# A fp32 encoder trunk on one core: the order of the matmuls in the MLP's first product, and where group C's query norm is applied

## The chip, the cores and the metric

One core of a Trainium2 chip runs the whole program. The metric is the device time of one execution in microseconds, lower is better; a kernel's time is the median of its runs.

## The reference, cut to what matters

Two layers (DEPTH 2) over one sequence of 256 tokens and a model width of 2048, all in float32:

```python
h = rmsnorm(x, norm_mix[l]); proj = h @ w_in[l]           # 2048 -> 3840: q, k, v of the groups A, B, C
oa = window_attention(...); ob = neighborhood_attention(...); oc = axial_global_attention(qc, kc, vc, ...)
x = x + concat(rmsnorm(oa), rmsnorm(ob), rmsnorm(oc)) @ w_o[l]
h = rmsnorm(x, norm_mlp[l])
u = relu(h @ w_up[l])                                       # 2048 -> 8192
x = x + (u * u) @ w_down[l]                                 # 8192 -> 2048

# group C: 16 query heads, 4 key heads, 64 wide
q = axial_rope(rmsnorm(q, q_gain), ...); k = axial_rope(rmsnorm(k, k_gain), ...)
p = softmax((q @ k.T) * 64 ** -0.5); o = p @ v
```

After the two layers a last rmsnorm follows. rmsnorm of a query head divides its 64 numbers by one root mean square, so it is one factor for each token and head.

## The kernel before, in words

Weights come from HBM in steps of 512 KB (`wraw`, 128 x 1024 elements). For each step ScalarE rounds them to `whi` (L803), VectorE takes the rest `wlo = wraw - whi` (L804), and TensorE runs products of the halves; activations are kept as a pair of halves too (`hT`, `hT2`, `mixT`, `uT`). The list `steps` sets the order of the weights: the input projection in eight chunks (`IN_CHUNKS`: qa, kva, kvc, qc0, qc1, vb, b0, b1), the output projection, then the MLP. Loads run seven steps ahead and splits two. Three of the products are run: high x high, high x low, low x high.

In the input and output projections and in the MLP's second product (`mode_b`, L449 to L451) the activations are the stationary operand and 512 weight columns stream: three matmuls of 512 columns for each 128 rows of weights. In the MLP's first product (`up_steps`) it is the other way round: a 128 x 128 block of weights is stationary and the tokens stream. One step has two k-blocks (`kk`) of 128 rows and four blocks of 128 output features (`fs`), each with a PSUM bank of its own (`box["b"][fs]`). For the high half of the weights both halves of the 256 tokens stream in one matmul of 512 columns (L614), and for the low half only the tokens' high half, 256 columns (L616), into the first 256 columns of the same bank. There are 8 steps for each of 16 feature chunks and 2 layers: 256 steps, 512 k-blocks, 2048 matmuls of each kind.

Attention is woven in between the weights' matmuls: a planner (`add`, `tick`) keeps pieces of work (`q_transposes` L246, `k_transposes` L261, `unit_scores` L324/L325, `unit_transp` L365, `unit_pv` L384/L377) with a cost and a delay in its own units, and releases them between steps. Its numbers do not change here. A unit is four heads by 128 queries; each layer has 8 units of C, 4 of A and 4 of B. The framework then settles each engine's order, which is fixed before the program runs; each engine works through its own list in order.

Group C's queries and keys go through `rope(raw, H, which, l, outs)` when their chunk of the projection ends: squares (L284) and their sums (L286) on VectorE; then, on GpSimd, mean plus epsilon (L288), the power -0.5 (`rsqrt`, L236), the product of `raw` with that factor (L291), and the rotary products with a cosine and a sine table (L297, L301), added at L509 into `qs`, which `q_transposes` reads. In a unit of C, VectorE takes the negative row maximum of the scores (L332), ScalarE the exponentials (L346), VectorE a reciprocal (L354) and GpSimd the product (L356).

Of the kernel before, what the change touches and what calls it, by code (L numbers as in the profile page):

```python
# [43 lines left out]
def tile_trunk(ctx: ExitStack, tc: tile.TileContext, x_in, w_in, w_o, w_up, w_down,  # L44
# [19 lines left out]
    def big(dt, *shape):  # L64
        return dp.tile([P, *shape], dt, tag="big", bufs=24, name=nm("big"))
# [168 lines left out]
    def rsqrt(ms, n):  # L234
        r = small(n)
        nc.gpsimd.tensor_tensor(r, ms, mhalf[:, 0:n], op=ALU.pow)  # L236
        return r
# [41 lines left out]
    def rope(raw, H, which, l, outs):  # L279

        n = NT * H
        sq = big(F32, NT * H * 64)
        flat = raw.rearrange("p t h d -> p (t h d)")
        nc.vector.tensor_mul(sq, flat, flat)  # L284
        s = small(n)
        nc.vector.tensor_reduce(s, sq.rearrange("p (a d) -> p a d", d=64), axis=AX.X, op=ALU.add)  # L286
        ms = small(n)
        nc.gpsimd.tensor_scalar(ms, s, 1.0 / 64, EPS, op0=ALU.mult, op1=ALU.add)  # L288
        r = rsqrt(ms, n)
        rv = raw.rearrange("p t h d -> p (t h) d")  # L290
        nc.gpsimd.tensor_mul(rv, rv, r.rearrange("p (a o) -> p a o", o=1).to_broadcast([P, n, 64]))  # L291
        t1 = big(F32, NT, H, 64)
        ct, st = ctab[which, l], stab[which, l]
        t2 = sq.rearrange("p (t h d) -> p t h d", t=NT, h=H)
        for t in range(NT):
            cb = ct[:, t:t + 1, :].to_broadcast([P, H, 64])
            nc.gpsimd.tensor_mul(t1[:, t, :, :], raw[:, t, :, :], cb)  # L297
            for a in range(4):
                b = a ^ 1
                sb = st[:, t:t + 1, 16 * a:16 * a + 16].to_broadcast([P, H, 16])  # L300
                nc.gpsimd.tensor_mul(t2[:, t, :, 16 * a:16 * a + 16], raw[:, t, :, 16 * b:16 * b + 16], sb)  # L301
            outs(t, t1[:, t, :, :], t2[:, t, :, :])


    class Unit:
# [12 lines left out]
    def unit_scores(u):  # L318
# [11 lines left out]
        if u.kind == "C":  # L330
            for b in range(2):
                nc.vector.tensor_reduce(negm[:, 2 * b:2 * b + 2], S[b], axis=AX.X, op=ALU.max, negate=True)  # L332
            src = [S[s // 2][:, s % 2, :] for s in range(4)]
        else:
            for b in range(2):
                nc.vector.scalar_tensor_tensor(p[:, 2 * b:2 * b + 2, :], S[b], 0.125,
                                               u.bias(b), op0=ALU.mult, op1=ALU.add)
            if u.kind == "A":
                nm0 = small(4)
                nc.vector.tensor_reduce(nm0, p, axis=AX.X, op=ALU.max, negate=True)  # L340
                nc.vector.tensor_tensor(negm, nm0, negsink[:, u.l, 4 * u.kv:4 * u.kv + 4], op=ALU.min)
            else:
                nc.vector.tensor_reduce(negm, p, axis=AX.X, op=ALU.max, negate=True)
            src = [p[:, s, :] for s in range(4)]
        for s in range(4):
            nc.scalar.activation(p[:, s, :], src[s], AF.Exp, bias=negm[:, s:s + 1],  # L346
                                 accum_out=sums[:, s:s + 1])
        if u.kind == "A":
            es = small(4)
# [105 lines left out]
    def layer_steps(l):  # L455
# [12 lines left out]
        def proj_evac(name, banks):  # L468
# [32 lines left out]
            elif name in ("qc0", "qc1"):  # L501
# [5 lines left out]

                def outs(t, a, b):
                    nc.gpsimd.tensor_add(qs[:, t, :].rearrange("p (h d) -> p h d", h=8), a, b)  # L509
                rope(raw, 8, "q", l, outs)  # L510
                i = int(name[2])
                kh, kl = st["k"]["C"]
                for g in range(2):
                    qT = big(F32R, 4, 256)
                    pq = add(lambda g=g, qT=qT: q_transposes(qs, 2 * g, qT), 0.45, delay=D_RQ)
                    for qb in range(2):
                        queue_unit(g_unit(l, st, "C", 2 * i + g, qb, qT, kh, kl, st["V"]["C"]), pq, st["kC"])
            elif name == "qa":
                qs = big(F32, NT, 512)
                for t in range(NT):  # L520
# [74 lines left out]
        def up_steps(g):  # L595
            for c in range(2):
                fc = 2 * g + c
                box = {}
                for k in range(8):
# [3 lines left out]
                    def mm(wh, wl, k=k, fc=fc, box=box):  # L603
# [2 lines left out]
                        ht = st["hT2"][k]  # L606
                        for kk in range(2):
                            for fs in range(4):
                                o = box["b"][fs]
                                s0 = k == 0 and kk == 0  # L610
                                s1 = k == 7 and kk == 1
                                sh = wh[:, kk, fs * P:(fs + 1) * P]
                                sl = wl[:, kk, fs * P:(fs + 1) * P]
                                nc.tensor.matmul(o.rearrange("p (s c) -> p s c", s=2), sh, ht[:, :, kk, :],  # L614
                                                 start=s0, stop=False, skip_group_check=True)
                                nc.tensor.matmul(o[:, 0:256], sl, ht[:, 0, kk, :],  # L616
                                                 start=False, stop=s1, skip_group_check=True)
                        if k == 7:
                            for b in range(2):

# [108 lines left out]
                                        ap=[[1, P], [512, 4], [1, 384]]))  # L729
        return tb  # L730

    def g_unit(l, st, kind, kv, qb, qT, kh, kl, V, bias=None):
        u = Unit()
        u.kind, u.l, u.kv, u.qb, u.qT, u.kh, u.kl, u.V = kind, l, kv, qb, qT, kh, kl, V
        u.slot = lambda s: (s, kv, qb)
        u.col = lambda s: s
# [224 lines left out]
```

## Time and profile before

| | |
|---|---|
| time, median of 3 runs (lowest to highest) | 2074.8 us (2074.34 to 2076.07) |
| the profiled execution: time, span | 2079.03 us, 2077.2 us |
| mean granted TensorE clock | 0.997 |
| PE busy | 2054.9 us, 99% of the span, 10423 matmuls |
| DVE, ACT, POOL busy | 1358.6, 1044.6, 274.4 us |
| DMA | 381.26 MB, mean 184 GB/s |

PE is TensorE's matmuls and PEld its weight loads, DVE is VectorE, ACT ScalarE, POOL GpSimd. The span runs from the first to the last instruction of the profiled execution. A matmul's recorded duration includes the time in which it fills and drains the array, and the next one starts before it ends, so what a matmul costs in a stream is the distance from its start to the next one's start, not its duration.

### The profile page before, as it was taken

The page shows a single profiled execution, that of the slowest core. Times are in us where ns is not written, and L with a number is a line of the kernel's source. Part 1 is how long each engine was busy: PE and PEld are TensorE (multiplying, and loading weights), DVE is VectorE, ACT ScalarE, POOL GpSimd, SP SyncE. Part 2 cuts the span into 40 slices and gives each one's busy share as a digit, 9 for nine tenths or more (in the row PEclk, how much of TensorE's full clock was granted, in tenths as well). Part 3 has the DMA queues.
Part 4 walks back from the last instruction along what each step waited for, and adds up shares of the span by engine and source line. Part 5 has one row for each costly group of instructions (what it writes and reads, how often), then busy time and mean ns, then how long its engine had stood idle before and what let it go on. Part 6 is the DMA issues. An engine that isn't in the chain of part 4 may idle for free.

```text
span 2077.2 us, 27421 instructions
## 1 busy us (share of the span) xinstructions
PE 2054.9 (99%) x10423; PEld 1739.5 (84%) x10423; DVE 1358.6 (65%) x1635; ACT 1044.6 (50%) x1538; POOL 274.4 (13%) x298
## 2 busy tenths in 40 slices
PE   9999999999999999999999999999999999999998
PEld 7878788888888888888888787888888888888887
DVE  6887976565565555656668889766565556656565
ACT  6657656444344443444556666555344444434444
POOL 0485420000000000000005843200000000000001
PEclk9999999999999999999999999999999999999999
DMA  7655465565666666566556453555666666666663
GB/s 283 180 159 152 152 193 174 189 191 187 193 186 190 191 189 193 186 193 189 186 183 184 148 163 118 193 173 190 191 186 193 192 185 192 190 190 188 192 212 123
DMA packets 107681, 381.26 MB, mean 184 GB/s; under 512 B 11891, under 2 KB 14707, under 8 KB 107548
## 3 DMA queue, kind: packets, MB, share of 16 engines
q1 hardware_dynamic: 107116, 378.41, 58.1%
q8 instruction: 82, 1.34, 0.3%
q10 hardware_dynamic: 432, 1.10, 0.1%
q14 instruction: 51, 0.42, 0.1%
HBM read 377.34 MB, written 2.11 MB: 183 GB/s over the span
## 4 chain that ended last, share of the span: by engine, by line
PE 92%; DVE 3%; POOL 3%; issue 1%; DMA 1%; ACT 1%; SPq 0%; POOLq 0%; DVEq 0%
PE mm L614 23%; PE mm L450 18%; PE mm L449 18%; PE mm L451 18%; PE mm L616 12%; PE tr L365 1%; DVE wlo L804 1%; PE tr L192 1%; PE mm L324 1%; PE mm L325 1%; POOL big L301 1%; DVE big L268 1%; POOL big L356 0%; POOL big L509 0%; DMA biasB<-in_rpb_dram 0%
## 5 line engine op out<-in xcount | busy, mean ns | idle before, releaser
L804 DVE TENSOR_TENSOR wlo<-wraw,whi 128x1024 fp32r<-128x1024 f32 (+1 forms) x697 | 867.2, 1246 | 654.8 <-ACT whi L803 652.3
L803 ACT CAST whi<-wraw 128x1024 fp32r<-128x1024 f32 (+1 forms) x697 | 730.1, 1050 | 914.3 <-PE mm L451 476.7
L614 PE MATMUL mm<-big,whi 128*128 128x512 f32 x2048 | 724.4, 399 | 0.0
L449 PE MATMUL mm<-whi,big 128*128 128x512 f32 (+1 forms) x1800 | 698.1, 389 | 2.4 <-ACT whi L803 1.4
L450 PE MATMUL mm<-wlo,big 128*128 128x512 f32 (+1 forms) x1800 | 695.7, 387 | 0.6 <-DVE wlo L804 0.4
L451 PE MATMUL mm<-whi,big 128*128 128x512 f32 (+1 forms) x1800 | 694.8, 386 | 0.0
L616 PE MATMUL mm<-big,wlo 128*128 128x256 f32 x2048 | 576.0, 281 | 0.0
L614 PEld LDWEIGHTS mm<-big,whi 128*128 128x128 f32 x2048 | 385.4, 188 | 95.2
L449 PEld LDWEIGHTS mm<-whi,big 128*128 128x128 f32 x1800 | 339.2, 189 | 68.7 <-DVE x L586 2.2
L451 PEld LDWEIGHTS mm<-whi,big 128*128 128x128 f32 x1800 | 339.2, 188 | 67.8
L450 PEld LDWEIGHTS mm<-wlo,big 128*128 128x128 f32 x1800 | 339.7, 189 | 66.2 <-DVE wlo L804 2.3
L616 PEld LDWEIGHTS mm<-big,wlo 128*128 128x128 f32 x2048 | 387.8, 189 | 0.5
L236 POOL TENSOR_TENSOR sm<-sm,mhalf 128x2 f32<-128x2 f32 (+3 forms) x16 | 23.7, 1482 | 785.9 <-DVE sm L231 772.0
L356 POOL TENSOR_SCALAR big<-big,sm 128x256 f32<-128x256 f32 x128 | 95.9, 767 | 224.4 <-DVE sm L354 199.7
L699 POOL TENSOR_TENSOR x<-x,big 128x512 f32<-128x512 f32 x6 | 8.6, 1453 | 722.7 <-ACT mid L706 722.7
L651 DVE SCALAR_TENSOR_TENSOR x<-mm,sm,x 128x512 f32<-128x512 f32 x127 | 89.2, 743 | 3.1 <-PE mm L451 3.1
L624 ACT COPY mid<-mm 128x256 f32<-128x256 f32 x128 | 46.7, 374 | 26.7 <-PE mm L616 26.7
L625 DVE TENSOR_TENSOR mid<-mid,mm 128x256 f32<-128x256 f32 x128 | 49.5, 420 | 0.0
L626 DVE SCALAR_TENSOR_TENSOR mid<-mid 128x512 f32<-128x512 f32 x64 | 44.0, 688 | 1.1
L630 DVE TENSOR_TENSOR big<-mid,big 128x512 fp32r<-128x512 f32 x64 | 43.8, 684 | 0.0
L367 DVE TENSOR_TENSOR big<-tr,big 128x512 fp32r<-128x512 f32 x64 | 41.1, 680 | 0.8 <-ACT big L366 0.5
L629 ACT CAST big<-mid 128x512 fp32r<-128x512 f32 x64 | 40.2, 627 | 2.6
(119 smaller groups left out, 1006.7 us busy)
## 6 DMA issues: line engine op xcount, KB each, us to landing
wraw<-in_w_up_dram SPq DMA_DIRECT2D x256, 512.0 KB, 3.5
wraw<-in_w_down_dram SPq DMA_DIRECT2D x256, 512.0 KB, 3.5
wraw<-in_w_in_dram SPq DMA_DIRECT2D x119, 512.0 KB, 3.6
wraw<-in_w_o_dram SPq DMA_DIRECT2D x64, 512.0 KB, 3.8
biasB<-in_rpb_dram SPq DMA_DIRECT2D x16, 349.5 KB, 6.3
biasA<-avec SPq DMA_DIRECT2D x4, 768.0 KB, 6.7
x<-in_x_dram SPq DMA_DIRECT2D x3, 512.0 KB, 8.7
big<-in_gfin_dram SPq DMA_DIRECT2D x2, 512.0 KB, 4.5
```

What stands on the lines that cost most here:

```text
L356: nc.gpsimd.tensor_scalar(p[:, s, :], p[:, s, :], rs[:, s:s + 1], 1.0, op0=ALU.mult, op1=ALU.mult)
L449: nc.tensor.matmul(o, a_h, wh[:, i, :], start=first and i == 0, stop=False)
L450: nc.tensor.matmul(o, a_h, wl[:, i, :], start=False, stop=False)
L451: nc.tensor.matmul(o, a_l, wh[:, i, :], start=False, stop=last and i == len(sub) - 1)
L614: nc.tensor.matmul(o.rearrange("p (s c) -> p s c", s=2), sh, ht[:, :, kk, :], start=s0, stop=False, skip_group_check=True)
L616: nc.tensor.matmul(o[:, 0:256], sl, ht[:, 0, kk, :], start=False, stop=s1, skip_group_check=True)
L624: nc.scalar.copy(ai, o[:, 256:512])
L625: nc.vector.tensor_add(ai, ai, o[:, 0:256])
L626: nc.vector.scalar_tensor_tensor(a, a, 0.0, a, op0=ALU.max, op1=ALU.mult)
L651: nc.vector.scalar_tensor_tensor(xs, box["b"][t], st["r2"][:, t:t + 1], xs, op0=ALU.mult, op1=ALU.add)
L803: last_hi[0] = nc.scalar.copy(h[:, part], w[:, part]).ins
L804: nc.vector.tensor_sub(lo[:, part], w[:, part], f(h[:, part]))
```

## The change

Three things. In `up_steps` each k-block first runs the four 512-column matmuls of its four feature blocks and then the four of 256 columns. In `rope` the squares are taken by an activation on ScalarE, for queries and keys. And for queries the factor r is no longer multiplied into `raw`: the rotary products are made of the raw queries, r is worked out behind them on GpSimd, is handed to the units as `rq`, and comes in at the softmax: the negative maximum is multiplied by it on VectorE, and the exponential takes it as its scale. Keys keep their order. `t2` gets a tile of its own, where it shared that of the squares.

```diff
@@ rope
-        nc.vector.tensor_mul(sq, flat, flat)
+        nc.scalar.activation(sq, flat, AF.Square, bias=zero1[:, 0:1])
         s = small(n)
         nc.vector.tensor_reduce(s, sq.rearrange("p (a d) -> p a d", d=64), axis=AX.X, op=ALU.add)
         ms = small(n)
-        nc.gpsimd.tensor_scalar(ms, s, 1.0 / 64, EPS, op0=ALU.mult, op1=ALU.add)
-        r = rsqrt(ms, n)
-        rv = raw.rearrange("p t h d -> p (t h) d")
-        nc.gpsimd.tensor_mul(rv, rv, r.rearrange("p (a o) -> p a o", o=1).to_broadcast([P, n, 64]))
+        if which == "k":
+            nc.gpsimd.tensor_scalar(ms, s, 1.0 / 64, EPS, op0=ALU.mult, op1=ALU.add)
+            r = rsqrt(ms, n)
+            rv = raw.rearrange("p t h d -> p (t h) d")
+            nc.gpsimd.tensor_mul(rv, rv, r.rearrange("p (a o) -> p a o", o=1).to_broadcast([P, n, 64]))
         t1 = big(F32, NT, H, 64)
+        t2 = big(F32, NT, H, 64)
...
+        if which == "k":
+            return
+        nc.gpsimd.tensor_scalar(ms, s, 1.0 / 64, EPS, op0=ALU.mult, op1=ALU.add)
+        r = sp.tile([P, n], F32, tag="rq", bufs=3, name=nm("rq"))
+        nc.gpsimd.tensor_tensor(r, ms, mhalf[:, 0:n], op=ALU.pow)
+        return r
@@ unit_scores, kind C
                 nc.vector.tensor_reduce(negm[:, 2 * b:2 * b + 2], S[b], axis=AX.X, op=ALU.max, negate=True)
+            nc.vector.tensor_mul(negm, negm, u.rq)
...
             nc.scalar.activation(p[:, s, :], src[s], AF.Exp, bias=negm[:, s:s + 1],
+                                 scale=u.rq[:, s:s + 1] if u.kind == "C" else 1.0,
                                  accum_out=sums[:, s:s + 1])
@@ up_steps
                         for kk in range(2):
                             for fs in range(4):
-                                o = box["b"][fs]
-                                s0 = k == 0 and kk == 0
-                                s1 = k == 7 and kk == 1
                                 sh = wh[:, kk, fs * P:(fs + 1) * P]
+                                nc.tensor.matmul(box["b"][fs].rearrange("p (s c) -> p s c", s=2), sh, ht[:, :, kk, :],
+                                                 start=k == 0 and kk == 0, stop=False, skip_group_check=True)
+                            for fs in range(4):
                                 sl = wl[:, kk, fs * P:(fs + 1) * P]
-                                nc.tensor.matmul(o.rearrange("p (s c) -> p s c", s=2), sh, ht[:, :, kk, :],
-                                                 start=s0, stop=False, skip_group_check=True)
-                                nc.tensor.matmul(o[:, 0:256], sl, ht[:, 0, kk, :],
-                                                 start=False, stop=s1, skip_group_check=True)
+                                nc.tensor.matmul(box["b"][fs][:, 0:256], sl, ht[:, 0, kk, :],
+                                                 start=False, stop=k == 7 and kk == 1, skip_group_check=True)
```

The changed kernel's lines stand 1 to 10 numbers further down: L614 and L616 of before are L621 and L625 there, and GpSimd's L297, L301 and L509 are L298, L302 and L518.

TensorE, the first k-block of the first MLP step, before (mm are the four banks, big the tokens, whi and wlo the halves of the weights):

```order
L614 MATMUL mm_3346<-big_3193,whi_3298 128x512
L616 MATMUL mm_3346<-big_3193,wlo_3299 128x256
L614 MATMUL mm_3347<-big_3193,whi_3298 128x512
L616 MATMUL mm_3347<-big_3193,wlo_3299 128x256
L614 MATMUL mm_3348<-big_3193,whi_3298 128x512
L616 MATMUL mm_3348<-big_3193,wlo_3299 128x256
L614 MATMUL mm_3349<-big_3193,whi_3298 128x512
L616 MATMUL mm_3349<-big_3193,wlo_3299 128x256
```

The same k-block in the changed kernel:

```order
L621 MATMUL mm_3355<-big_3202,whi_3307 128x512
L621 MATMUL mm_3356<-big_3202,whi_3307 128x512
L621 MATMUL mm_3357<-big_3202,whi_3307 128x512
L621 MATMUL mm_3358<-big_3202,whi_3307 128x512
L625 MATMUL mm_3355<-big_3202,wlo_3308 128x256
L625 MATMUL mm_3356<-big_3202,wlo_3308 128x256
L625 MATMUL mm_3357<-big_3202,wlo_3308 128x256
L625 MATMUL mm_3358<-big_3202,wlo_3308 128x256
```

The eight matmuls and their sizes are the same; four of a size now stand together, and consecutive matmuls write different banks.

GpSimd, from a unit's last product to the end of the rope of qc0 in the first layer, before (sm are small tiles, big the queries and the rotary products):

```order
L356 TENSOR_SCALAR big_1015<-big_1015,sm_1031 128x256 x4
L288 TENSOR_SCALAR sm_1107<-sm_1105 128x16
L236 TENSOR_TENSOR sm_1109<-sm_1107,mhalf 128x16
L291 TENSOR_TENSOR big_1099<-big_1099,sm_1109 128x1024
L297 TENSOR_TENSOR big_1112<-big_1099,ctab_q_447 128x512
L301 TENSOR_TENSOR big_1103<-big_1099,stab_q_448 128x8x16 x4
L297 TENSOR_TENSOR big_1112<-big_1099,ctab_q_447 128x512
L509 TENSOR_TENSOR big_1102<-big_1112,big_1103 128x512
L301 TENSOR_TENSOR big_1103<-big_1099,stab_q_448 128x8x16 x4
L509 TENSOR_TENSOR big_1102<-big_1112,big_1103 128x512
```

The same place in the changed kernel:

```order
L365 TENSOR_SCALAR big_1016<-big_1016,sm_1032 128x256 x4
L298 TENSOR_TENSOR big_1109<-big_1100,ctab_q_447 128x512
L302 TENSOR_TENSOR big_1110<-big_1100,stab_q_448 128x8x16 x4
L298 TENSOR_TENSOR big_1109<-big_1100,ctab_q_447 128x512
L518 TENSOR_TENSOR big_1103<-big_1109,big_1110 128x512
L302 TENSOR_TENSOR big_1110<-big_1100,stab_q_448 128x8x16 x4
L518 TENSOR_TENSOR big_1103<-big_1109,big_1110 128x512
L306 TENSOR_SCALAR sm_1108<-sm_1106 128x16
L308 TENSOR_TENSOR rq_1124<-sm_1108,mhalf 128x16
```

The mean and the power have moved behind the last sum that the transposes read, and the 128x1024 product is gone.

VectorE at the same time, before (wlo is the low half of a step's weights, L286 the sums of squares):

```order
L354 RECIPROCAL sm_1031<-sm_1017 128x4
L284 TENSOR_TENSOR big_1103<-big_1099 128x1024
L804 TENSOR_TENSOR wlo_1202<-wraw_987,whi_1201 128x1024
L286 TENSOR_REDUCE sm_1105<-big_1103 128x16
L804 TENSOR_TENSOR wlo_1230<-wraw_1037,whi_1229 128x1024
L804 TENSOR_TENSOR wlo_1264<-wraw_1081,whi_1263 128x1024
L397 TENSOR_TENSOR mid_1062<-tr_1181,ot_1186 64x2x128
```

And in the changed kernel:

```order
L363 RECIPROCAL sm_1032<-sm_1018 128x4
L814 TENSOR_TENSOR wlo_1203<-wraw_988,whi_1202 128x1024
L286 TENSOR_REDUCE sm_1106<-big_1104 128x16
L814 TENSOR_TENSOR wlo_1231<-wraw_1038,whi_1230 128x1024
L376 TENSOR_TENSOR big_1149<-tr_1150,big_1148 128x512
L376 TENSOR_TENSOR big_1149<-tr_1157,big_1148 128x512
L814 TENSOR_TENSOR wlo_1265<-wraw_1082,whi_1264 128x1024
```

The squares have left VectorE, and the third split stands behind the unit's low halves of the probabilities (L367 of before) instead of ahead of them.

More of the change, by code (lines that the diff above doesn't have):

```diff
@@ L516, in proj_evac @@
                     for qb in range(2):
-                        queue_unit(g_unit(l, st, "C", 2 * i + g, qb, qT, kh, kl, st["V"]["C"]), pq, st["kC"])
+                        c0 = qb * 8 + 4 * g
+                        queue_unit(g_unit(l, st, "C", 2 * i + g, qb, qT, kh, kl, st["V"]["C"],
+                                          rq=rq[:, c0:c0 + 4]), pq, st["kC"])
             elif name == "qa":
@@ L730, in bias_a, with g_unit @@
         return tb
-    def g_unit(l, st, kind, kv, qb, qT, kh, kl, V, bias=None):
+    def g_unit(l, st, kind, kv, qb, qT, kh, kl, V, bias=None, rq=None):
         u = Unit()
+        u.rq = rq
         u.kind, u.l, u.kv, u.qb, u.qT, u.kh, u.kl, u.V = kind, l, kv, qb, qT, kh, kl, V
```

3 lines of the change are left out of this document (1 added, 2 removed).

## Prediction

> **What bounds the kernel now.** I read the page's busy times first, then the chain of work that ended last, then TensorE's groups by line, and then TensorE's timeline, because on an engine that is never idle only the distances between starts say what a matmul costs.
>
> ```profile
> PE 2054.9 (99%) x10423; PEld 1739.5 (84%) x10423; DVE 1358.6 (65%) x1635; ACT 1044.6 (50%) x1538; POOL 274.4 (13%) x298
> PE mm L614 23%; PE mm L450 18%; PE mm L449 18%; PE mm L451 18%; PE mm L616 12%; PE tr L365 1%; DVE wlo L804 1%; PE tr L192 1%; PE mm L324 1%; PE mm L325 1%; POOL big L301 1%; DVE big L268 1%; POOL big L356 0%; POOL big L509 0%; DMA biasB<-in_rpb_dram 0%
> L614 PE MATMUL mm<-big,whi 128*128 128x512 f32 x2048 | 724.4, 399 | 0.0
> L616 PE MATMUL mm<-big,wlo 128*128 128x256 f32 x2048 | 576.0, 281 | 0.0
> ```
>
> TensorE is the bound: 99% busy, and the chain is its matmuls (L449 to L451 in `mode_b`, L614 and L616 in the MLP's first product). L614 and L616 never find the engine idle, so in the MLP only the pace of the stream can change. The rest can change where TensorE waits.
>
> **Part 1, the MLP's order.** TensorE's timeline, around the end of an MLP group (start, duration):
>
> ```profile
> 772.34 0.39 PE L614 MATMUL mm<-big,whi 128*128 128x512 f32 x1
> 772.57 0.28 PE L616 MATMUL mm<-big,wlo 128*128 128x256 f32 x1
> 772.69 0.40 PE L614 MATMUL mm<-big,whi 128*128 128x512 f32 x1
> ...
> 774.46 0.40 PE L614 MATMUL mm<-big,whi 128*128 128x512 f32 x1
> ...
> 776.93 0.40 PE L449 MATMUL mm<-whi,big 128*128 128x512 f32 x1
> ...
> 777.88 0.39 PE L450 MATMUL mm<-wlo,big 128*128 128x512 f32 x1
> ...
> 779.72 0.39 PE L449 MATMUL mm<-whi,big 128*128 128x512 f32 x1
> ...
> 780.85 0.39 PE L451 MATMUL mm<-whi,big 128*128 128x512 f32 x1
> ```
>
> Six pairs from 772.34 to 774.46 make 0.3533 us a pair, so a k-block of four pairs costs 1.413 us. Later, five matmuls of 512 from 779.72 to 780.85 make 0.226 each. So a pair costs 0.127 beyond a settled 512, where half of 0.226 would be 0.113. And the 512s right behind the pairs are slow at first: four from 776.93 to 777.88 take 0.95, 0.237 each.
>
> What do four of 256 in a row cost, and four of 512 behind them? The nearest rows are a unit's scores, eight matmuls of 256 between 512s:
>
> ```profile
> 64.62 0.28 PE L324 MATMUL mm<-mid,big 128*128 128x256 f32 x1
> 64.73 0.28 PE L325 MATMUL mm<-mid,big 128*128 128x256 f32 x1
> ...
> 65.57 0.40 PE L449 MATMUL mm<-whi,big 128*128 128x512 f32 x1
> ...
> 66.50 0.39 PE L450 MATMUL mm<-wlo,big 128*128 128x512 f32 x1
> ```
>
> The first 256 takes 0.11 and the other seven (64.73 to 65.57) 0.12 each; the next four 512s take 0.93 (65.57 to 66.50), 0.2325 each, slower than 0.226 but not as slow as 0.237. A short matmul thus leaves the next few 512s slower. Is it instead L614's streamed operand, two pieces of 256 tokens, that makes it slow? Its first matmul behind settled 512s says no:
>
> ```profile
> 642.93 0.39 PE L614 MATMUL mm<-big,whi 128*128 128x512 f32 x1
> 643.15 0.28 PE L616 MATMUL mm<-big,wlo 128*128 128x256 f32 x1
> ```
>
> It takes 0.22, like any other. So the grouped k-block costs 0.93 for four 512s and 0.47 to 0.48 for four 256s (the first between 0.11 and 0.12, three at 0.12): 1.407 with the middle, 6.3 ns less than 1.413. Times 512 k-blocks: -3.2 us. Behind each of the 16 groups of up steps (8 a layer) the second product starts slow: 12 matmuls from 776.93 to 779.72 take 2.79, 0.07 more than 12 at 0.2265; behind four 256s I expect 0.03 more (0.93 against 4 x 0.2265), so 16 x 0.04 = -0.6 us. Sum of part 1: -3.8 us.
>
> The bounds. If 512s settled at once, a block would be 4 x 0.2265 + 0.11 + 3 x 0.12 = 1.376: -37 ns, -19 us; no row shows them settle at once. If they behaved as behind the long alternation, 0.95 + 0.48 = 1.43: +17 ns, +8.7 us. I take the middle row, since it is the only one of 512s behind a run of 256s.
>
> What hides the rest: the low halves are needed four matmuls later than now, never earlier; the first bank of a step is finished later by about 3 x (0.353 - 0.12) = 0.7 us, and the next chunk writes four other banks, so nobody waits for it.
>
> Here the Trainium skill speaks against the gain. "TensorE: Matmul & The Clock Gate", section Back-to-back issue gap, gives a gap of N / 2.4 + 2.5 ns for N columns, whatever stands beside it. By it a pair would be an estimated 215.8 + 109.2 = 325 ns in either order and part 1 would be worth 0. The trace disagrees in size (353 for the pair) and in form, since the same 512 columns take 0.22, 0.2325 or 0.237 by what ran before.
>
> **Part 2, the query's norm.** The view of waits on TensorE, then its timeline at the longest one in each layer:
>
> ```profile
> PE tr L246 <- POOL big L509: 5.5, 2, 2.8
> PE tr L384 <- DVE big L367: 1.8, 4, 0.6
> ```
>
> ```profile
> 125.94 0.27 PE L246 MATMUL tr<-ident,big 128*128 128x128 f32 x1
> 128.98 1.75 PE L246 MATMUL tr<-ident,big 128*128 128x128 f32 x7 [2.77 <-POOL big L509]
> 130.38 0.77 PE L449 MATMUL mm<-whi,big 128*128 128x512 f32 x1
> ...
> 132.17 0.40 PE L450 MATMUL mm<-wlo,big 128*128 128x512 f32 x1
> 1154.73 0.27 PE L246 MATMUL tr<-ident,big 128*128 128x128 f32 x1
> 1157.76 0.98 PE L246 MATMUL tr<-ident,big 128*128 128x128 f32 x7 [2.76 <-POOL big L509]
> ...
> 1159.51 0.39 PE L450 MATMUL mm<-wlo,big 128*128 128x512 f32 x1
> ```
>
> The query transposes of qc0 wait for GpSimd's last rotary sum. In the second layer the first transpose starts 3.03 before the second (1154.73, 1157.76) instead of 0.11: 2.92 lost. Up to the fifth 512 that is 4.78, so 1.86 of work. In the first layer the same work takes 125.94 to 132.17, 6.23: 4.37 lost, since after the stop the matmuls run at half pace (four of 512 from 130.38 to 132.17, 0.45 each). Together 7.3 us.
>
> GpSimd's timeline ahead of that wait in the first layer:
>
> ```profile
> 105.22 3.88 POOL L356 TENSOR_SCALAR big<-big,sm 128x256 f32<-128x256 f32 x4 [10.88 <-DVE sm L354]
> 109.18 1.05 POOL L288 TENSOR_SCALAR sm<-sm 128x16 f32<-128x16 f32 x1
> 110.32 3.76 POOL L236 TENSOR_TENSOR sm<-sm,mhalf 128x16 f32<-128x16 f32 x1
> 114.15 2.15 POOL L291 TENSOR_TENSOR big<-big,sm 128x1024 f32<-128x1024 f32 x1
> 116.38 1.35 POOL L297 TENSOR_TENSOR big<-big,ctab_q 128x512 f32<-128x512 f32 x1
> ...
> 126.80 2.12 POOL L509 TENSOR_TENSOR big<-big,big 128x512 f32<-128x512 f32 x1
> ```
>
> The mean, the power and the 128x1024 product stand from 109.18 to 116.38, 7.2 us ahead of the rotary products, which then take 12.54 (to 128.92). Without them the rotary products start when L356 ends, at 109.1, and end at 121.7, 4.2 us before TensorE comes to the transposes at 125.94. So the whole wait goes, -7.3 us. What is late next: the factor, at 121.7 + 1.05 + 3.76 = 126.6. The units' scores follow the transposes by a planned delay, so rq is there first; a VectorE multiply that waited for it would hold back the weight splits behind it.
>
> The small terms. The squares leave VectorE (L284, 1.23 each) and come to ScalarE, where twice their length in L183's rate bounds them:
>
> ```profile
> L284 DVE TENSOR_TENSOR big<-big 128x1024 f32<-128x1024 f32 x4 | 4.9, 1226 | 1.5 <-ACT big L504 1.5
> L183 ACT ACTIVATE mid<-x,zero 128x512 f32<-128x512 f32 x32 | 22.9, 721 | 0.6 <-DVE x L586 0.6
> L624 ACT COPY mid<-mm 128x256 f32<-128x256 f32 x128 | 46.7, 374 | 26.7 <-PE mm L616 26.7
> L346 ACT ACTIVATE big<-mm,sm 128x256 f32<-128x256 f32 x64 | 29.5, 474 | 23.6 <-DVE sm L332 23.2
> L350 DVE TENSOR_TENSOR sm<-sm,negsink 128x4 f32<-128x4 f32 x8 | 2.0, 246 | 0.3
> ```
>
> Between 0.72 and 1.44 each, once for a chunk, while weights are split two steps ahead; the split behind it comes that much later, and nothing waits for it within two steps. The multiply of the maximum costs VectorE about 0.25 (L350) sixteen times, 4 us in all, against the 4.9 that the four query squares take: about even. A per-row scale costs the exponential about 0.10 (L346 with a per-row bias 474, L624 without any 374), 64 times 6.4 us of ScalarE, which is 50% busy. TensorE's own waits for these two engines are short (1.8 us for L367); a new order there can shorten or lengthen them. I take 0, with ends of -2 and +3 us.
>
> **Sum.** -3.8 - 7.3 + 0 = -11.1 us. The profiled execution took 2079.03 (span 2077.2), 0.2% above the median of 2074.8; the terms are differences, so I take them off the median: 2063.7 us. About 0.2% (4.1 us) is what a measurement of this kernel can tell from no change.
>
> **The rivals.**
> - The order does not matter (part 1 is 0): -7.3, 2067.5. For it: matmuls of one size cost the same in most rows. Against: 0.2325 and 0.237 for 512. The Trainium skill's formula above is this rival; no row has its 325 ns.
> - The wait only moves: the transposes get their queries, but ScalarE's longer list or VectorE's factor makes the splits late and 5 of the 7.3 come back: 2068.7. Against: 4.2 us and two steps of slack.
> - 512s settle faster behind four 256s than behind eight: with a block at 1.387, -26 ns or -13 us, 2053.9. For it: the pace recovers by itself within twelve matmuls; against: five to eight 256s were enough for 0.2325.
> - Slower: four short matmuls in a row drive the next 512s to the slowest pace, and four are too few to recover. The slowest is at most a pair less the shortest 256, 0.353 - 0.11 = 0.243; with 0.48 for the 256s a block is 1.452, +39 ns or +20 us, with -7.3 a total of 2087.5. It decides (slower than 2078.9) from a block of 1.436 on, that is (7.3 + 4.1) us over 512 blocks above 1.413. For it: the pace behind the long alternation is 0.237; against: the run of eight leaves 0.2325.
>
> **Chances.** Forecast 0.58 (its own range 2058 to 2067); order does not matter 0.15; the wait only moves 0.10; faster settling 0.09; slower mechanism 0.05 in full, and 0.03 for a half of it that just eats the gain. The first four are all beyond 0.2% faster, less 0.08 for weaker versions that end within it: faster 0.84, same 0.11, slower 0.05. The range 2054 to 2071 holds all but the slower mechanism and the far end of faster settling.
>
> **What would show it.** The eight matmuls of a k-block (L621, L625) should take 1.40 to 1.41 us from first start to first start, with 512s near 0.2325 and 256s near 0.12; L246 should have no wait for GpSimd's last sum, with no half-paced 512s behind it; VectorE's new multiply should not wait for rq. I am wrong if a block stays at 1.413 or exceeds it, or if new waits for L803/L804 stand where L246's wait was.

## The result, and the profile after

The changed kernel takes 2064.3 us (median of 5 runs, 2062.96 to 2067.51), beside 2076.07 us (2074.34 to 2076.87) for the kernel before on the same chip: a ratio of 0.9945, 95% interval 0.9931 to 0.9960, or about 11.5 us. The forecast was 2063.7 us, -11.1 us from its median of before. The profiled execution took 2062.96 us with a span of 2061.2.

The page of the changed kernel: busy times, the chain that ended last by line, and two groups (operation, shape, count, then busy us and mean ns, then idle time in front).

```profile
PE 2042.5 (99%) x10423; PEld 1735.7 (84%) x10423; DVE 1338.7 (65%) x1645; ACT 1048.1 (51%) x1544; POOL 254.9 (12%) x294
PE mm L621 23%; PE mm L459 19%; PE mm L458 19%; PE mm L460 19%; PE mm L625 12%; PE tr L374 1%; PE tr L393 1%; PE mm L331 1%; PE tr L192 1%; PE mm L332 1%; PE tr L386 0%; DVE big L417 0%; DMA x<-in_x_dram 0%; PE tr L246 0%; DVE big L268 0%
L621 PE MATMUL mm<-big,whi 128*128 128x512 f32 x2048 | 559.1, 394 | 0.0
L625 PE MATMUL mm<-big,wlo 128*128 128x256 f32 x2048 | 325.7, 281 | 0.0
```

TensorE is still the bound, and GpSimd's sums and products have gone from the chain. The busy times of L621 and L625 mislead: they fell from 724.4 and 576.0 to 559.1 and 325.7 (from 1300 to 885 us) while the MLP won 5 us. Matmuls overlap in the records, and neighbours of one line are counted once where they do; here only starts tell the pace. TensorE's timeline of the changed kernel in the MLP's first product (start, duration, count):

```profile
559.72 1.09 PE L621 MATMUL mm<-big,whi 128*128 128x512 f32 x4
560.65 0.64 PE L625 MATMUL mm<-big,wlo 128*128 128x256 f32 x4
561.13 1.09 PE L621 MATMUL mm<-big,whi 128*128 128x512 f32 x4
562.06 0.63 PE L625 MATMUL mm<-big,wlo 128*128 128x256 f32 x4
```

Four 512s take 0.93, four 256s 0.48, a block 1.41. The mean over the starts of 496 blocks is 1403.3 ns, and 1413.6 before.

TensorE's waits (us in total, times, longest):

```profile
PE mm L458 <- DVE big L253: 3.8, 2, 1.9
...
PE mm L459 <- DVE wlo L814: 0.9, 2, 0.5
```

The wait of L246 for GpSimd is gone, and a wait that was not there before, of L458 for VectorE's L253, is the longest.

Where the time went is read from the starts at which TensorE enters and leaves a stretch. The kernel before (L614 opens the MLP, L449 follows its last first product in layer 1):

```profile
330.40 0.48 PE L614 MATMUL mm<-big,whi 128*128 128x512 f32 x1
...
954.52 0.40 PE L449 MATMUL mm<-whi,big 128*128 128x512 f32 x1
...
1357.69 0.48 PE L614 MATMUL mm<-big,whi 128*128 128x512 f32 x1
```

The changed kernel at the same three places:

```profile
322.95 0.48 PE L621 MATMUL mm<-big,whi 128*128 128x512 f32 x1
...
944.38 0.40 PE L458 MATMUL mm<-whi,big 128*128 128x512 f32 x1
...
1344.33 0.48 PE L621 MATMUL mm<-big,whi 128*128 128x512 f32 x1
```

| stretch | before | after | difference | forecast |
|---|---|---|---|---|
| start to the MLP of layer 1 | 330.40 | 322.95 | -7.45 | -4.4 |
| layer 1's last first product to the MLP of layer 2 | 403.17 | 399.95 | -3.2 | -2.9 |
| all first products (512 blocks and, in each layer, eight transposes L192 among them), summed from starts | 725.22 | 720.06 | -5.2 | -3.2 |
| second products behind them | no change | | 0 | -0.6 |

That is 16 us between the two profiled executions, more than the 11.8 between the medians. Some 2.7 us of it is not the change's: the windows view (window, length, busy PE and count, granted clock, DMA share, GB/s) of the start, before:

```profile
11.00:15.00 4.00, 4.00 (x12) 0.50 1.04 416
```

and after, with the columns of all engines ahead of the clock:

```profile
10.90:15.00 4.10, 4.10 (x20) 3.35 (x20) 2.09 (x3) 3.29 (x8) 0.00 (x0) 1.00 1.04 415
```

The same code ran at a granted clock of 0.50 in the one execution and 1.00 in the other: the same matmul (L451 of before, L460 of after) starts at 16.57 and at 13.90. Without that, layer 1 won 4.8 us. Of these, some 1.45 are the half-paced matmuls that stood behind the old stop in this execution of before (the prediction's 4.37 against 2.92 us in layer 2).

### The profile page after: what moved, and what is told of

Same layout as the page of the kernel before. It is cut to its first block, busy times and chain, and to the rows that moved or that the text cites. A ratio compares the mean times of both kernels' runs of the same rounds, so it can differ in the third digit from the quotient of the medians.

```text
span 2061.2 us, 27437 instructions
## 1 busy us (share of the span) xinstructions
PE 2042.5 (99%) x10423; PEld 1735.7 (84%) x10423; DVE 1338.7 (65%) x1645; ACT 1048.1 (51%) x1544; POOL 254.9 (12%) x294
## 4 chain that ended last, share of the span: by engine, by line
PE 97%; DVE 1%; ACT 1%; issue 1%; DMA 0%; SPq 0%; DVEq 0%; POOLq 0%; POOL 0%; ACTq 0%
PE mm L621 23%; PE mm L459 19%; PE mm L458 19%; PE mm L460 19%; PE mm L625 12%; PE tr L374 1%; PE tr L393 1%; PE mm L331 1%; PE tr L192 1%; PE mm L332 1%; PE tr L386 0%; DVE big L417 0%; DMA x<-in_x_dram 0%; PE tr L246 0%; DVE big L268 0%
## 5 line engine op out<-in xcount | busy, mean ns | idle before, releaser
L458 PE MATMUL mm<-whi,big 128*128 128x512 f32 (+1 forms) x1800 | 695.2, 387 | 5.2 <-DVE big L253 3.8
L459 PE MATMUL mm<-wlo,big 128*128 128x512 f32 (+1 forms) x1800 | 693.5, 385 | 0.9 <-DVE wlo L814 0.9
L460 PE MATMUL mm<-whi,big 128*128 128x512 f32 (+1 forms) x1800 | 692.9, 385 | 0.0
L621 PE MATMUL mm<-big,whi 128*128 128x512 f32 x2048 | 559.1, 394 | 0.0
L458 PEld LDWEIGHTS mm<-whi,big 128*128 128x128 f32 x1800 | 338.1, 188 | 70.0 <-issue 4.1
L460 PEld LDWEIGHTS mm<-whi,big 128*128 128x128 f32 x1800 | 338.2, 188 | 67.4
L459 PEld LDWEIGHTS mm<-wlo,big 128*128 128x128 f32 x1800 | 338.5, 188 | 66.1 <-DVE wlo L814 1.8
L621 PEld LDWEIGHTS mm<-big,whi 128*128 128x128 f32 x2048 | 350.8, 189 | 47.7
L625 PEld LDWEIGHTS mm<-big,wlo 128*128 128x128 f32 x2048 | 314.2, 189 | 43.5
L625 PE MATMUL mm<-big,wlo 128*128 128x256 f32 x2048 | 325.7, 281 | 0.0
L365 POOL TENSOR_SCALAR big<-big,sm 128x256 f32<-128x256 f32 x128 | 87.5, 704 | 245.0 <-DVE sm L363 188.8
L236 POOL TENSOR_TENSOR sm<-sm,mhalf 128x2 f32<-128x2 f32 (+2 forms) x12 | 12.4, 1030 | 780.8 <-DVE sm L231 767.3
L354 ACT ACTIVATE big<-mm,sm,rq 128x256 f32<-128x256 f32 x64 | 35.3, 561 | 22.7 <-DVE sm L340 17.0
```

What stands on the lines that cost most here:

```text
L365: nc.gpsimd.tensor_scalar(p[:, s, :], p[:, s, :], rs[:, s:s + 1], 1.0, op0=ALU.mult, op1=ALU.mult)
L458: nc.tensor.matmul(o, a_h, wh[:, i, :], start=first and i == 0, stop=False)
L459: nc.tensor.matmul(o, a_h, wl[:, i, :], start=False, stop=False)
L460: nc.tensor.matmul(o, a_l, wh[:, i, :], start=False, stop=last and i == len(sub) - 1)
L621: nc.tensor.matmul(box["b"][fs].rearrange("p (s c) -> p s c", s=2), sh, ht[:, :, kk, :], start=k == 0 and kk == 0, stop=False, skip_group_ ...
L625: nc.tensor.matmul(box["b"][fs][:, 0:256], sl, ht[:, 0, kk, :], start=False, stop=k == 7 and kk == 1, skip_group_check=True)
```

## The experiments

Each kernel was timed beside the kernel before on the same chip; ratios are to it, with 95% intervals. Two questions: do the parts add up as the prediction's sum had it, and what sets the pace of the MLP's matmuls?

### The MLP's order alone

```diff
-  for fs in range(4): 512 columns of bank fs; 256 columns of bank fs
+  for fs in range(4): 512 columns of bank fs
+  for fs in range(4): 256 columns of bank fs
```

(the queries' norm as before)

> The kernel before with only the MLP's new order (four matmuls of 512 columns, then four of 256). Theory 1 (a short matmul leaves the next 512s slower, so fewer changes from short to long are cheaper): a k-block takes 1.403 us as in the changed kernel, against 1.413 before; 512 blocks x 10.2 ns = -5.2 us, ratio 0.9975, and the wait of L246 for GpSimd (2.8 us twice) stays. Theory 2 (the order of the sizes is worth nothing by itself and all of the gain is the query norm's): ratio 1.000.

Measured: 2072.54 us beside 2076.6, ratio 0.9979 (0.9971 to 0.9988), so -4.4 us with an interval of -6.0 to -2.5. A block is 1403.3 ns as in the changed kernel, and the old wait is still there:

```profile
PE tr L246 <- POOL big L509: 5.6, 2, 2.8
```

The order is worth its 5.2 us of starts by itself.

### The whole norm part, with the MLP as before

```diff
-  512 and 256 grouped in the MLP
+  512 and 256 alternating, as before
```

(against the changed kernel)

> The kernel before with only the attention edits (squares on ScalarE, query norm in the exponential), the MLP in the old order. Theory 1: the blocks stay at 1.413 us, the wait of L246 is gone (-7.3 us), and by the changed kernel's profile the rest of the attention is about even; -6 to -8 us, ratio 0.9965. Theory 2: the full -11.8 us, ratio 0.9945.

Measured: 2069.03 us, ratio 0.9959 (0.9947 to 0.9972), -8.5 us (-11.0 to -5.8). 0.9979 x 0.9959 = 0.9938, within the interval of the full change: the MLP and the norm add up. The waits are those of the changed kernel (L458 for L253 3.7 us in all), so the new wait belongs to the norm part.

### Only the squares on ScalarE

```diff
-        nc.vector.tensor_mul(sq, flat, flat)
+        nc.scalar.activation(sq, flat, AF.Square, bias=zero1[:, 0:1])
```

> The kernel before with only the squares of queries and keys on ScalarE instead of VectorE. If the squares on VectorE are what makes L384 wait for L367 behind qc0 (0.69 us a layer), that wait goes and the wait of L246 shrinks by at most the 1.2 us of a square: -1 to -3 us. If they cost as much on ScalarE by late weight splits: 0. The wait of L246 for GpSimd must stay above 1.5 us a layer, since the mean, the power and the 128x1024 product (7.2 us) still stand ahead of the rotary products.

Measured: 2080.43 us, ratio 1.0011 (1.0002 to 1.0020), about +2.3 us. TensorE's timeline at the old wait in layer 1, and GpSimd's last sum there:

```profile
125.07 0.27 PE L246 MATMUL tr<-ident,big 128*128 128x128 f32 x1
128.51 1.60 PE L246 MATMUL tr<-ident,big 128*128 128x128 f32 x7 [3.17 <-POOL big L509]
```

```profile
127.19 1.26 POOL L509 TENSOR_TENSOR big<-big,big 128x512 f32<-128x512 f32 x1
```

TensorE comes to the transposes 0.87 us earlier than before (125.07, 125.94), most of it since a wait of L384 for VectorE ahead of them went. But GpSimd's chain ends at 128.45, only 0.5 us earlier than before, so TensorE waits 3.17 instead of 2.77: half of what is saved ahead of the wait is paid in it. In layer 2 ten 512s behind this stop ran at 427 ns, which the profiled run of before did not have there; with the slow transposes ahead of them that is an estimated 2.7 us in these two profiles. The +2.3 us of the medians probably has the same source, since the mean granted clock was 0.9963 over this kernel's ten runs and 0.9980 over the 27 runs of the kernel before beside them; no run shows it directly.

### Only the norm in the exponential, squares on VectorE

```diff
-        nc.scalar.activation(sq, flat, AF.Square, bias=zero1[:, 0:1])
+        nc.vector.tensor_mul(sq, flat, flat)
```

(against the whole norm part)

> The kernel before with only the query norm put into the exponential; the squares stay on VectorE, the MLP in the old order. If the norm's place alone makes the gain: the wait of L246 is gone as in the changed kernel, -5 to -8 us, the wait of L384 at qc0 (0.69 us a layer) stays. If the squares' move was needed for it: L246 still waits for GpSimd.

Measured: 2076.76 us, ratio 1.0001 (0.9992 to 1.0011): nothing. The waits of L246 are gone here too, yet the time is not. TensorE's waits:

```profile
PE mm L458 <- DVE big L253: 3.8, 2, 1.9
PE tr L393 <- DVE big L376: 2.4, 2, 1.2
```

L331 waits 0.8 us for L253 besides. Against the whole norm part (L393 1.1, L331 not at all) that is 2.1 us more, all for VectorE, and in this execution the stop before L458 is followed by half-paced matmuls in both layers:

```profile
225.56 0.28 PE L332 MATMUL mm<-big,big 128*128 128x256 f32 x1
227.72 0.47 PE L458 MATMUL mm<-whi,big 128*128 128x512 f32 x1 [1.88 <-DVE big L253]
...
229.07 0.63 PE L460 MATMUL mm<-whi,big 128*128 128x512 f32 x1
229.50 0.63 PE L458 MATMUL mm<-whi,big 128*128 128x512 f32 x1
```

Each stands 0.43 behind the last instead of 0.227. This kernel and the whole norm part run the same matmuls in the same order, so their starts can be set side by side: TensorE falls 7.6 us behind in the deferral alone, 4.1 of it mostly around the stops of L331 and L393, 3.1 at the two half-paced stretches and 0.3 at the start.

So the two halves of the norm part don't add up in the medians, +2.3 and 0 alone against -8 together, but part of this gap is the clock: its mean was 0.9967 over the deferral's ten runs and 0.9984 over the five of the whole norm part. In layer 2's attention stretch (403.17 before, 405.7 with the squares alone, 403.5 with the deferral alone, 399.9 with both) the half-paced matmuls are worth an estimated 2.7 us with the squares alone and 1.6 with the deferral alone. Without them the stretch changes by -0.2 and -1.3 alone and by -3.3 together: the halves still don't add up, by less than the medians say. The deferral takes away GpSimd's wait and makes VectorE the next one that is late; the squares' move gives VectorE the time back that this needs.

### Up matmuls in pairs: two of 512, two of 256

Theory 1 is that of the prediction: short matmuls slow the 512s behind them, and a longer run lets them recover. Theory 2 blames the PSUM bank that neighbours share.

```diff
-  512 of banks 0 1 2 3, 256 of banks 0 1 2 3
+  512 of 0 1, 256 of 0 1, 512 of 2 3, 256 of 2 3
```

> The changed kernel with its eight matmuls of an up block in groups of two and two (512, 512, 256, 256) instead of four and four. Theory 1 (a 512-column matmul behind short ones needs three or four of its own size to come back to 227 ns; in the changed kernel the four stand 234.6, 234.4, 231.9 and 228.3 ns apart): no 512 gets past its second place, so 2 x 234.5 + 117.4 + 119.6 = 706 ns for four matmuls, 1.412 us for eight, the whole gain of the MLP order is gone (+4.5 us on the changed kernel's 2064.3, about 2069). Theory 2 (the old order is slow because each 256 writes the PSUM bank that the 512 ahead of it has just written): consecutive matmuls write different banks here too, 1.403 us, no change, 2064.

Measured: 2059.53 us, ratio 0.9926 (0.9911 to 0.9941), faster than either theory allowed. TensorE's timeline:

```profile
559.74 0.62 PE L622 MATMUL mm<-big,whi 128*128 128x512 f32 x2
560.20 0.40 PE L626 MATMUL mm<-big,wlo 128*128 128x256 f32 x2
560.43 0.63 PE L622 MATMUL mm<-big,whi 128*128 128x512 f32 x2
560.90 0.39 PE L626 MATMUL mm<-big,wlo 128*128 128x256 f32 x2
561.13 0.63 PE L622 MATMUL mm<-big,whi 128*128 128x512 f32 x2
```

A block takes 1.39 us (mean 1393.9 ns), 9.4 ns less than in fours (1403.3). By position, the starts stand 233.0, 230.8, 113.4, 119.2, 233.3, 235.8, 115.9 and 112.5 ns apart. Theory 1 as I held it is wrong: it charged a run of two 234.5 for each 512, which is nearly right (233.2), and 118.5 for each 256, which is not (115.2).

### Nearly alternating, but never the same bank twice

```diff
-  512 of 0 1 2 3, 256 of 0 1 2 3
+  512 of 0, 512 of 1, 256 of 0, 512 of 2, 256 of 1, 512 of 3, 256 of 2, 256 of 3
```

> The changed kernel with the eight matmuls of an up block in the order 512 of bank 0, 512 of bank 1, 256 of bank 0, 512 of bank 2, 256 of bank 1, 512 of bank 3, 256 of banks 2 and 3: the sizes alternate nearly as before the change, but no two neighbours write one bank. Theory 1 (run lengths of one size decide): 1.411 to 1.414 us for eight, 2068 to 2070. Theory 2 (the bank of the neighbour decides): 1.403 us, 2064.

Measured: 2070.57 us, ratio 0.9970 (0.9960 to 0.9981). From one block's start to the next:

```profile
561.01 0.63 PE L622 MATMUL mm<-big,whi 128*128 128x512 f32 x2
...
562.43 0.40 PE L622 MATMUL mm<-big,whi 128*128 128x512 f32 x1
```

1.42 (mean 1413.4 ns), as alternating (1413.6). Banks of their own give nothing: theory 2 falls.

### Pairs, all four in one bank

```diff
+  for fs in range(4): 512 of both k-blocks, then 256 of both k-blocks, all into bank fs
```

> The changed kernel with up matmuls in groups of two and two (512, 512, 256, 256), but all four of a group into one PSUM bank: both k-blocks of one bank, then the next bank. Theory P (only the order of sizes counts, and pairs are the cheap one): 1.394 us for eight as in the run with pairs in two banks, 2059.5. Theory B (pairs are cheap because neighbours write different banks): back to 1.403 to 1.413 us, 2064 to 2069.

Measured: 2060.22 us, ratio 0.9920 (0.9907 to 0.9934).

```profile
559.97 0.63 PE L621 MATMUL mm<-big,whi 128*128 128x512 f32 x2
...
561.36 0.40 PE L621 MATMUL mm<-big,whi 128*128 128x512 f32 x1
```

1.39 again; the 512 blocks take 715.24 us in all, to the hundredth as with two banks. Of the two, the order of sizes decides, and the bank does not.

### Eight and eight

```diff
+  for kk in range(2): four of 512
+  for kk in range(2): four of 256
```

> The changed kernel with the two k-blocks of a step taken together: eight 512-column matmuls, then eight of 256. Theory 1: the first four 512s 234.6 + 234.4 + 231.9 + 228.3, four more at 226.7; the 256s 117.4 + 119.6 + 118.8 + 5 x 118.4: 2.784 us for sixteen instead of 2 x 1.403, -23 ns x 256 steps = -5.8 us, 2058.5. Theory 2: 2.807 us, no change, 2064. Under either, the wait of the out-projection matmul L458 for L253 (3.8 us) stays.

Measured: 2062.54 us, ratio 0.9931 (0.9918 to 0.9943).

```profile
561.10 2.00 PE L621 MATMUL mm<-big,whi 128*128 128x512 f32 x8
562.94 1.11 PE L626 MATMUL mm<-big,wlo 128*128 128x256 f32 x8
563.89 1.09 PE L621 MATMUL mm<-big,whi 128*128 128x512 f32 x4
```

Sixteen matmuls take 2.79 (mean 2792.7 ns; theory 1 said 2784). The 512s reach 226.7 at the sixth, and the 256s stand 113.3 and 119.2, then 120.0 six times. So there are two costs with opposite signs:

| order | eight matmuls, ns | mean 512 | mean 256 |
|---|---|---|---|
| alternating (before) | 1413.6 | 236.5 | 116.9 |
| 2, 1, 1, 1, 1, 2 (own banks) | 1413.4 | 235.6 | 117.7 |
| four and four (the change) | 1403.3 | 232.3 | 118.5 |
| eight and eight, half of it | 1396.4 | 230.0 | 119.1 |
| two and two | 1393.9 | 233.2 | 115.2 |

From alternating over fours to eights, the longer the runs, the cheaper a 512 and the dearer a 256; pairs don't fit this row, for in them a 256 costs least, and a 512 little more than in fours. Why pairs are so good for the 256s is open: the starts show no rule by position, and no run here tests one.

### The low product over 384 columns

The old alternating order, with the low product streaming 192 tokens of both halves.

```diff
-  256 columns: tokens 0 to 255 of half 0
+  384 columns: tokens 0 to 191 of both halves
```

> The changed kernel in its old up order (512, then the low product into the same bank), but the low product streams 384 columns (192 tokens of each half) instead of 256, so the outputs of the MLP differ: the low product is left out for 64 tokens of one half and added for 192 of the other. Theory A (a 512 is slow behind a matmul that streams for no longer than a weight load, about 108 ns): behind a stream of 384 columns the 512 is back at 226.7 ns, the 384 at three quarters of that, 170: 397 ns for a pair, 1.588 us for eight, 94 us more than the changed kernel, about 2159. Theory B (any change of size or of weights between halves costs it): the 512 stays at 233 to 235 ns, the 384 at 175 or more, 409 ns for a pair, 1.636 us, about 2183.

Measured: 2178.08 us, ratio 1.0492 (1.0478 to 1.0506).

```profile
599.79 0.40 PE L625 MATMUL mm<-big,whi 128*128 128x512 f32 x1
...
601.41 0.40 PE L625 MATMUL mm<-big,whi 128*128 128x512 f32 x1
```

Four pairs take 1.62 (mean 1627.1 ns): 231.3 to 232.6 for the 512, 175.0 for the 384. Theory A wanted 1.588, with the 512 back at 226.7. Behind a stream half as long again as 256 it takes 231.8 on average instead of 236.5, so about half of the slowness stays, and a stream too short to hide a weight load isn't all of it. (No run here shows the load of 108 ns that theory A went by: a load's record is 188 ns long, but 256s with a load each start 113 to 120 ns apart.) Theory B is near (1.636).

### The new wait: C's transposes earlier (12 and 18 instead of 24)

Both on the version with pairs. The wait is TensorE's L458 for VectorE; in the changed kernel it looks like this:

```profile
222.40 0.28 PE L332 MATMUL mm<-big,big 128*128 128x256 f32 x1
224.56 0.47 PE L458 MATMUL mm<-whi,big 128*128 128x512 f32 x1 [1.89 <-DVE big L253]
```

with VectorE's timeline beside it:

```profile
220.77 2.23 DVE L417 SCALAR_TENSOR_TENSOR big<-mid,gn,big 128x256 fp32r<-128x256 f32 x2
223.02 1.39 DVE L253 TENSOR_TENSOR big<-tr,big 64x512 fp32r<-64x512 f32 x2
```

L458 begins a step, takes the next of eight PSUM banks in turn, and that bank holds transposed queries until L253 has read them; VectorE comes to L253 late, behind L417 and the weight split ahead of it.

```diff
-    D_RQ = 24.0
+    D_RQ = 12.0   (and 18.0)
```

> The version with pairs (512, 512, 256, 256) in which the plan's delay between C's query and its transposes (D_RQ) is 12 instead of 24, so that the transposes L246 and their halves L253 come some 30 to 60 matmuls earlier. Theory 1 (the new wait of L458 is the price of the place where the plan puts the transposes: VectorE reaches L253 late, behind L814 and L417, and the bank comes free late): the 3.7 us of L458 go, nothing of that size comes, ratio to before 0.9926 - 0.0018 = 0.991, about 2056. Theory 2 (VectorE's backlog is the cause, whatever the place): another wait of 1 to 2 us in each layer, 2059 to 2060.

> As the version with delay 12, with D_RQ 18: the transposes stand some 50 matmuls earlier in layer 1 than with 24, between two projection steps, and L253 stands ahead of L417 on VectorE. Theory 1: the wait goes, about 2056. Theory 2: 2059 to 2060.

Measured: 2085.36 us with 12, ratio 1.0039 (1.0027 to 1.0052), and 2064.15 with 18, 0.9938 (0.9924 to 0.9951). TensorE's waits with 12:

```profile
PE tr L246 <- POOL big L518: 15.9, 6, 4.0
```

and with 18:

```profile
PE tr L246 <- ACT big L482: 3.6, 2, 1.8
PE tr L246 <- POOL big L518: 2.9, 2, 1.5
```

L458's wait is indeed gone, but theory 1 was wrong in what it moved: the queries that hold the bank are B's, not C's. C's transposes now come before GpSimd's rotary sums (L518) and wait for those: 2.9 us of that wait are back with 18, beside 3.6 for ScalarE's L482 (it copies B's queries), and 15.9 with 12. The norm is out of the path of the transposes, but the rotary products are still in it: of 12, 18 and 24 only 24 left no wait there.

### The new wait: B's transposes later (8 instead of 6)

```diff
-                pq = add(lambda: q_transposes(qs, 0, qT), 0.45, delay=D_QK)
+                pq = add(lambda: q_transposes(qs, 0, qT), 0.45, delay=8.0)
-                pk = add(lambda: k_transposes(qs, 2, 2, kh, kl), 0.45, delay=D_QK)
+                pk = add(lambda: k_transposes(qs, 2, 2, kh, kl), 0.45, delay=8.0)
```

> The version with pairs (512, 512, 256, 256) in which the plan's delay between B's projections and their transposes is 8 instead of 6 (C's stays 24). The transposes L246 and L261 of b1, whose half L253 frees the PSUM bank that L458 waits for, then stand after the next step's twelve projection matmuls and the scores L331 instead of before them, and the bank that L458 takes in the rotation is another. Theory 1 (the new wait is the price of that one place and of the bank's turn in the rotation): L458's 3.7 us for L253 go and nothing of their size comes: ratio 0.9926 - 0.0018 = 0.991, about 2056. Theory 2 (VectorE is behind by that much at this place, and whichever matmul comes next meets it): a wait of 1 to 2 us in each layer stands elsewhere, or the units of b1 end later, 2059 to 2061.

Measured: 2059.06 us, ratio 0.9918 (0.9904 to 0.9932), as with pairs alone. TensorE's waits:

```profile
PE mm L459 <- DVE wlo L815: 3.7, 4, 1.4
```

The 3.7 us of L458 for L253 are gone, and L459 waits longer for the low halves of its weights, 3.7 us where it was 0.9; the attention stretch of layer 2 takes 400.0 us (399.7 with pairs alone). Theory 2 holds at the two places tried: VectorE is late by that much here, and what TensorE asks of it next meets that.

The version with pairs in the MLP and the full norm change (2059.53 us) is faster than both kernels. Its median is 4.8 us below the changed kernel's; the intervals of the two ratios overlap, but the starts of the 512 blocks don't vary: 715.24 us in each of the five kernels with pairs, 720.06 in both with fours.

## Why the prediction was right

**Part 1, the MLP's order (-3.8 forecast; -5.2 by starts, -4.4 timed).** For fours the mechanism was the one named: a 512 is dearer behind short matmuls, and the row of scores gave the price of both sizes well, 0.2325 against a mean of 232.3 ns and 0.12 against 118.5. It is not the whole rule, since by it pairs would have lost the gain, and they nearly doubled it. The term was mis-sized, since the rows have steps of 10 ns: I put the block at 1.407, and it is 1.4033, 10.3 ns under before instead of 6.3. The second term, -0.6 for the second product, did not come. From the first 512 behind the four 256s to the next first product in the changed kernel:

```profile
590.60 0.40 PE L458 MATMUL mm<-whi,big 128*128 128x512 f32 x1
...
634.16 0.61 PE L621 MATMUL mm<-big,whi 128*128 128x512 f32 x2
```

43.56 us, and before, from 776.93 (shown in the prediction) to

```profile
820.51 0.39 PE L614 MATMUL mm<-big,whi 128*128 128x512 f32 x1
```

43.58. Faster settling behind four 256s was thus wrong, for the rival and for this term. The formula in the Trainium skill, "TensorE: Matmul & The Clock Gate", section Back-to-back issue gap, made the order worth nothing; the runs disagree, with 1394 to 1414 ns for the same eight matmuls. That section gives the formula for a single isolated matmul, and the prediction set it against a stream.

**Part 2, the query's norm (-7.3 forecast).** TensorE at the transposes of qc0 in both layers, after:

```profile
122.52 1.03 PE L246 MATMUL tr<-ident,big 128*128 128x128 f32 x8
...
1143.86 1.03 PE L246 MATMUL tr<-ident,big 128*128 128x128 f32 x8
```

All eight without a stop, and behind them the 512s at full pace. GpSimd's last sum and the factor in layer 1:

```profile
115.57 2.36 POOL L518 TENSOR_TENSOR big<-big,big 128x512 f32<-128x512 f32 x1
...
119.24 2.91 POOL L308 TENSOR_TENSOR rq<-sm,mhalf 128x16 f32<-128x16 f32 x1
```

The sum ends at 117.93, 4.6 us before TensorE comes (4.2 forecast), the factor at 122.15 (126.6 forecast), before any scores. The stretches won 3.2 us in layer 2 (2.9 forecast) and 4.8 in layer 1 (4.4), which includes the half pace behind the old stop. That part, 1.45 of the 7.3, the prediction read from one execution and booked as certain. It isn't: behind the same stop the matmuls ran at half pace in both layers of the MLP's order alone, and in layer 1 only of the kernel before; and the new stops of L458 are followed by half pace in some executions too (last section).

**The small terms (0 forecast, ends -2 and +3).** Their sum is about -0.7 us (-0.3 and -0.4 beyond part 2), so 0 was a good number, but by luck. They are not small and independent: a wait of L384 of 0.3 us a layer goes, the waits for VectorE around B's units that went (L449 for x, L324, L450 and the rest of L384) are replaced by those of L458, L393 and L459, and the sum depends on both halves of the edit: alone, the deferral measures as nothing. "What is late next" is answered wrongly in the prediction: it named the factor, and it is VectorE's queue of weight splits and halves. The rival in which the wait only moves came true for the deferral alone, and the squares' move, which I priced as a cost to hide, averted most of it. The exponential's per-row scale costs 87 ns (474 to 561 in the group of L354), near the 100 forecast, on an engine that had the time.

**The sum.** That 11.1 and the measured 11.8 between the medians lie so close is in part luck. Without the stretches at half clock the profiles give 5.2 + 3.3 + 3.2 = 11.7 us. The mean granted clock of the runs is the same, 0.998, for the changed kernel and for the 27 runs of the kernel before beside the first experiments, so little of the gain between medians should be the clock. The 1.45 us of half pace that the forecast counted too much and the 1.4 us that it missed in the MLP then offset each other, and the rest is the 0.7 us of the small terms.

## What to carry to other kernels

When the work behind a wait is taken away, ask which engine is late next and move load off that engine in the same edit; here each half alone measured as nothing or as a loss. On an engine that never idles, read the distance between starts, not busy time, and try two or three orders of the same matmuls: sizes in pairs were worth twice the gain of fours here. Moving a wait to another place by the plan's delays won nothing here, where the engine waited for had the same work ahead of it.

## What the hardware showed that I had not expected

- The pace of a matmul depends on what ran before it. A 512 takes 226.7 ns settled; for up to five matmuls behind short ones it takes 224 to 241 by position, 230 to 237 on average over an order. A 256 takes 112.5 to 120.0 ns by position: 113.3 at the head of a run of eight and 120.0 at its end. The bank makes no difference, and a stream of 384 instead of 256 ahead halves a 512's excess without removing it.
- After a stop TensorE may run at half pace, or not, for the same code. Behind the same stop of L458 for L253 (2.16 and 2.15 us between starts), the windows view of the deferral alone and of the whole norm part (columns as in the section on the result):

```profile
228.70:231.50 2.80, 2.80 (x8) 2.19 (x7) 2.73 (x5) 0.56 (x2) 0.00 (x0) 0.52 0.42 153
```

```profile
225.50:229.00 3.50, 3.50 (x16) 2.90 (x16) 3.43 (x6) 1.98 (x4) 0.74 (x1) 1.00 0.70 220
```

  The granted clock is 0.52 in the one and 1.00 in the other, with 0.427 and 0.227 us between 512s. The seven profiles that have this stop with both halves of the norm part (the changed kernel, the whole norm part, pairs, pairs in one bank, own banks, eights, 384 columns) have it 14 times, with half pace behind it in 4; behind the longer stop of L246 for GpSimd (idle 2.8 to 3.2 us: before, the MLP's order alone, the squares alone) it came 5 times in 6. Such a stretch lasts 3.4 us, or 6.8, and costs about 1.6 us or more. The Trainium skill, "TensorE: Matmul & The Clock Gate", Part 1, has a gate that halves the clock by a free-running window of activity, so that the same kernel gets more or fewer slow matmuls from run to run. The trace agrees in the halving and in its variation: the start of the profiled executions has 0.50 and 1.00 for the same code. A difference of 2 us between two single profiles of this kernel can be that alone.
